# Two gated MLPs whose down-projection takes 16 of 22 row blocks in seven block products instead of eight

## The chip, the cores and the metric

The kernel runs on one core of one Trainium2 chip. A core has five engines with queues of their own: the matrix engine (PE, with its weight loads PEld), the vector engine VectorE (DVE), the scalar engine ScalarE (ACT), GpSimd (POOL), and SyncE (SP), which here only issues DMAs. Operands lie in the on-chip memory SBUF, matmul results in the eight banks of PSUM. The metric is the device time of one execution, in microseconds (us); lower is better.

## The reference

The reference is a trunk of two layers on one sequence of 512 tokens with 1024 features, in float32. Each layer has a mixer, a cross-attention into 256 memory rows, and a gated MLP; each is followed by x <- LayerNorm(alpha * x + f(x)). The change touches the MLP, whose hidden width D_FF is 2816, or 22 blocks of 128:

```python
def conv_ffn(x, w_up, conv_w, conv_b, w_down):
    up = x @ w_up
    a, g = up[..., :D_FF], up[..., D_FF:]
    g = causal_dwconv(g, conv_w) + conv_b
    return (jax.nn.gelu(g) * a) @ w_down
```

Layer 0 mixes with a spatial gate and trailing pooling (`mixer_ab`), layer 1 with a short gated convolution (`mixer_c`).

## The kernel before

**Numbers as pairs.** Every matmul operand is held as a high and a low part in a shorter format (float32r). `split` (L68) makes them: ScalarE copies the value into the high part (L70), VectorE subtracts it from the value for the low part (L71). `mm3` (L132) multiplies two such operands with three matmuls: high x high, high x low, low x high (L133 to L135).

**Weights.** They pass through in chunks of 128 x 1024, 512 KB, in the order of a list written out beforehand, `plan` (L81 to L96). `Weights.load` (L104) takes a raw buffer (4 of them), lets SyncE load the chunk (L117) and splits it into one of 6 ring places (`RING`). `take` hands out the next chunk; `done` (L126), called when the matmuls of a chunk have been written out, loads one more into the oldest place.

**Matmul forms.** In `proj_feat` (L163) weights stand still and activations move, and the result has features on the partitions. In `proj_tok` (L182) the activations stand still, 128 x 128 at a time, and 512 columns of the weights move; the result has tokens on the partitions. The MLP's up-projection uses the first form, its down-projection the second.

**MLP.** The 22 hidden blocks are worked in three groups, `FFN_GROUPS` = 6, 8 and 8 blocks. For a group, `ffn_up` (L500) takes two chunks for each hidden block m (gate and value), runs 24 matmuls for each, and then convolves (ScalarE L371, VectorE L373 twice), applies gelu (ScalarE L509), multiplies (VectorE L510) and splits into the pair of tiles of `Act`. Then `residual_norm` (L229) multiplies the group with its rows of `ffn_w_down`: for each of two column halves n, four PSUM banks, one for each block of 128 tokens, collect the group's blocks, and four additions on VectorE (L246) add them into x, with alpha in the first group. A chunk of `ffn_w_down` covers two row blocks and one column half.

**The last part of a product.** In the last group (`final`) the second column half goes token block by token block: all chunks of that half are held, each token block's products run, are added to x, and the row is normalised (`normalise`, L192: statistics on VectorE, a power on GpSimd in L198, two passes on VectorE in L199 and L201) while the next token block multiplies. Transposes back to feature form (`to_feat`, L218) of the first two token blocks stand inside the products of the third and fourth; those of the last two are emitted by `late` in the next stage. In the last layer the fourth token block is cut into halves of 256 columns, and the rows go out by DMA (L203).

**Order.** Nothing is synchronised by hand. A tile library assigns buffers, places semaphores, and orders each engine's queue; the code's order is its guide. Pools: 11 pairs of activation tiles, 6 ring places, 4 raw buffers, 9 temporaries of 512 columns, 8 PSUM banks.

Of the kernel before, what the change touches and what calls it, by code (L numbers as in the profile page):

```python
# [8 lines left out]
F32 = mybir.dt.float32  # L9
# [5 lines left out]
P = 128  # L15
# [14 lines left out]
RING = 6  # L30
FFN_GROUPS = ((0, 6), (6, 14), (14, 22))
# [4 lines left out]
def kernel(ctx: ExitStack, tc: tile.TileContext, a: dict, out: bass.AP):  # L36
# [24 lines left out]

    def duo(tag="act"):
        pool = apool if tag == "act" else wpool
        h = pool.tile([P, CH], F32R, tag=tag + "h", name=nm(tag + "h"))
        l = pool.tile([P, CH], F32R, tag=tag + "l", name=nm(tag + "l"))
        return h, l

    def split(h, l, src):  # L68
        """h + l == src exactly, each with 12 significant bits."""
        nc.scalar.copy(h, src)  # L70
        nc.vector.tensor_sub(l, src, h.bitcast(F32))  # L71

    def load_split(src, tag):
        raw = rpool.tile([P, CH], F32, tag="raw", name=nm("raw"))
        nc.sync.dma_start(raw, src)
        h, l = duo(tag)
        split(h, l, raw)
        return h, l

    # ---- the weights' chunks, in the order in which the tensor engine meets them  # L80
    plan = []  # L81
    for layer in range(2):
# [11 lines left out]
        for m0, m1 in FFN_GROUPS:  # L94
            plan += [("ffn_w_up", layer, i) for i in range(2 * m0, 2 * m1)]
            plan += [("ffn_w_down", layer, n, i) for n in range(2) for i in range(m0 // 2, m1 // 2)]  # L96

    class Weights:
        """A ring of chunks: take() gives the next one, and done() loads one more in place of the oldest."""

        def __init__(self):
            self.ready, self.loaded, self.taken = [], 0, 0

        def load(self, parts=1, other=None):  # L104
            """Loads a chunk; in parts that alternate with those of other = (source, duo), if it is given."""
# [6 lines left out]
            raws = [rpool.tile([P, CH], F32, tag="raw", name=nm("raw")) for _ in both]  # L112
# [19 lines left out]
    def mm3(ps, lh, ll, rh, rl, start, stop):  # L132
        nc.tensor.matmul(ps, lh, rh, start=start, stop=False)  # L133
        nc.tensor.matmul(ps, lh, rl, start=False, stop=False)  # L134
        nc.tensor.matmul(ps, ll, rh, start=False, stop=stop)  # L135

    # ---- constants
# [11 lines left out]
    wsT = cpool.tile([P, 4, P], F32, tag="wsT", name="wsT")  # L149
    bsb = cpool.tile([P, 4, P], F32, tag="bsb", name="bsb")  # L150

    # ---- activations held as (high, low) pairs, one pair of tiles for two blocks of 128 features
# [9 lines left out]

    def proj_feat(ps, w, xT, cols=slice(0, S)):  # L163
        """ps[features, tokens] = w.T @ xT, w a chunk [P, 8, 128] of the weight's columns."""
# [4 lines left out]
    def proj_batch(keys, xT, late=None):  # L169
        """proj_feat for a few chunks; late() emits the last half of the tokens in xT."""  # L170
# [21 lines left out]
    def normalise(z, stats, g, b, dst=None):  # L192
        """z = (z - mean) * rsqrt(var + eps) * g + b over the free axis."""
# [11 lines left out]
    def load_consts():  # L205
        nc.sync.dma_start(wsT, a["sgu_w"])
# [6 lines left out]
        for t in range(NT):  # L213
            nc.sync.dma_start(xt[t], a["x"][0, t * P : (t + 1) * P, :])

    xt = [xpool.tile([P, D], F32, tag=f"x{t}", name=f"x{t}", bufs=1) for t in range(NT)]

    def to_feat(xT, t):  # L218
        """xT[:, :, block t] = transpose of xt[t]."""
# [8 lines left out]

    def residual_norm(groups, wname, ln, layer, last=False, hooks={}, ahead=None):  # L229
        """x = LayerNorm(alpha * x + sum over groups of act.T @ w), as (transposed x, function that  # L230
        emits the last half of its tokens).
# [381 lines left out]
```

## Time and profile before

| | |
|---|---|
| median of 3 runs | 1361.77 us (1361.37 to 1362.26) |
| span of the profiled execution, first to last instruction | 1359.5 us |
| instructions | 16304 |
| matmuls recorded | 6628 |
| bytes loaded on SyncE's queue | 141.94 MB |

The profile is a record of one execution; the page lists only its span, and the runs' median lies 2.3 us above it. Its views: the page's busy times of each engine and its 40 slices; the chain of work that ended last; the groups of instructions by line, operation and shape, each with count, busy time, mean duration in ns, and the idle time of the engine ahead of it with what ended it; the waits, with total, count and longest; stretches, which give each engine's busy time between two instants; and timelines, which list start, duration, engine, line, tiles and shapes. In a name such as `wl<-raw,wh` the output stands left of the arrow; `wh` and `wl` are the two parts of a ring place, `acth` and `actl` of an activation, `ps` is a PSUM bank, `x` the residual stream. A few per cent of the matmul records may be missing.

### The profile page before, as it was taken

How to read it: one execution, taken by the hardware profiler on the slowest of the kernel's cores; microseconds unless marked ns; L12 is line 12 of the kernel's file. 1: busy time of each engine (PE TensorE's matmuls, PEld its weight loads, DVE VectorE, ACT ScalarE, POOL GpSimd, SP SyncE). 2: the span in 40 equal slices, each digit the busy share in tenths (PEclk: the TensorE clock that was granted, in tenths of full speed). 3: DMA queues.
4: the chain of work that ended last, by engine and by line, in shares of the span. 5: the costliest groups of instructions: out<-in, count | busy, mean ns of one | idle time of the engine just before them, and what ended most of it. 6: DMA issues, size and time to landing. Idle time of an engine off the chain costs nothing.

```text
span 1359.5 us, 16304 instructions
## 1 busy us (share of the span) xinstructions
PE 1347.2 (99%) x6628; PEld 1143.2 (84%) x6628; DVE 736.5 (54%) x998; ACT 465.3 (34%) x663; POOL 48.6 (4%) x68
## 2 busy tenths in 40 slices
PE   8999999999999999999999999999999999999997
PEld 7888888898888888888988888988898888888886
DVE  5768446675444424446744447565674444444436
ACT  5343345234223313332532222354243233313320
POOL 0102000010000000001000001000110000000001
PEclk9999999999999999999999999999999999999999
DMA  8633533133332233332623331442143233332301
GB/s 283 207 124 108 171 120 114 62 104 114 97 105 93 93 97 105 94 93 93 217 93 94 101 101 47 158 152 78 47 153 95 94 98 104 93 93 98 104 32 62
DMA packets 42844, 149.28 MB, mean 110 GB/s; under 512 B 5136, under 2 KB 5264, under 8 KB 42768
## 3 DMA queue, kind: packets, MB, share of 16 engines
q1 hardware_dynamic: 41040, 141.94, 32.7%
q0 software_dynamic: 1728, 6.29, 1.3%
q8 instruction: 52, 0.85, 0.2%
q14 instruction: 24, 0.20, 0.0%
HBM read 146.12 MB, written 2.10 MB: 109 GB/s over the span
## 4 chain that ended last, share of the span: by engine, by line
PE 99%; DMA 0%; DVE 0%; POOLq 0%; DVEq 0%; ACT 0%; issue 0%; SPq 0%
PE ps L133 32%; PE ps L134 32%; PE ps L135 32%; PE ps L223 1%; PE ps L469 1%; PE ps L346 0%; DMA raw<-in_ab_w_v 0%; POOLq L601 0%; DVE x L201 0%; DVEq L601 0%; ACT wh L70 0%; DVE stats L254 0%; DVE x L246 0%; SPq L117 0%; DVE mv L196 0%
## 5 line engine op out<-in xcount | busy, mean ns | idle before, releaser
L71 DVE TENSOR_TENSOR wl<-raw,wh 128x1024 fp32r<-128x1024 f32 (+1 forms) x251 | 304.3, 1212 | 416.7 <-ACT wh L70 406.8
L133 PE MATMUL ps<-acth,wh 128*128 128x512 f32 (+1 forms) x1316 | 478.5, 364 | 0.0
L134 PE MATMUL ps<-actl,wh 128*128 128x512 f32 (+1 forms) x1316 | 478.0, 363 | 0.0
L135 PE MATMUL ps<-acth,wl 128*128 128x512 f32 (+1 forms) x1316 | 478.0, 363 | 0.0
L70 ACT CAST wh<-raw 128x1024 fp32r<-128x1024 f32 (+1 forms) x251 | 262.2, 1045 | 607.6 <-PE ps L134 276.3
L133 PE MATMUL ps<-wh,acth 128*128 128x512 f32 (+1 forms) x712 | 277.3, 390 | 4.6 <-ACT wh L70 4.6
L133 PEld LDWEIGHTS ps<-acth,wh 128*128 128x128 f32 x1316 | 248.4, 189 | 38.9
L135 PEld LDWEIGHTS ps<-acth,wl 128*128 128x128 f32 x1316 | 248.4, 189 | 38.9
L134 PEld LDWEIGHTS ps<-actl,wh 128*128 128x128 f32 x1316 | 248.4, 189 | 38.6
L135 PE MATMUL ps<-wh,actl 128*128 128x512 f32 (+1 forms) x712 | 276.1, 388 | 0.0
L134 PE MATMUL ps<-wl,acth 128*128 128x512 f32 (+1 forms) x712 | 276.0, 388 | 0.0
L133 PEld LDWEIGHTS ps<-wh,acth 128*128 128x128 f32 x712 | 134.1, 188 | 31.5 <-ACT wh L70 4.6
L135 PEld LDWEIGHTS ps<-wh,actl 128*128 128x128 f32 x712 | 134.0, 188 | 27.5
L134 PEld LDWEIGHTS ps<-wl,acth 128*128 128x128 f32 x712 | 134.2, 188 | 27.2 <-DVE wl L71 0.4
L70 ACT CAST acth<-ps 128x256 fp32r<-128x256 f32 (+1 forms) x144 | 63.0, 470 | 121.4 <-PE ps L223 81.9
L198 POOL TENSOR_TENSOR rs<-rs,mhalf 128x1 f32<-128x1 f32 x28 | 40.2, 1437 | 1290.1 <-DVE rs L197 1290.1
L71 DVE TENSOR_TENSOR actl<-ps,acth 128x256 fp32r<-128x256 f32 (+1 forms) x144 | 73.0, 536 | 14.0 <-ACT acth L70 13.6
L510 DVE TENSOR_TENSOR tmp<-tmp,ps 128x512 f32<-128x512 f32 x44 | 30.3, 688 | 80.6 <-PE ps L135 79.2
L246 DVE SCALAR_TENSOR_TENSOR x<-x,ps 128x512 f32<-128x512 f32 (+1 forms) x81 | 54.6, 678 | 31.9 <-PE ps L135 31.6
L373 DVE SCALAR_TENSOR_TENSOR tmp<-ps,convw,tmp 128x511 f32<-128x511 f32 x88 | 65.7, 746 | 1.5
L509 ACT ACTIVATE tmp<-tmp 128x512 f32<-128x512 f32 x44 | 27.8, 632 | 85.9 <-DVE tmp L373 85.9
L70 ACT CAST acth<-tmp 128x512 fp32r<-128x512 f32 x64 | 39.4, 620 | 20.0 <-DVE tmp L330 14.0
(66 smaller groups left out, 549.2 us busy)
## 6 DMA issues: line engine op xcount, KB each, us to landing
raw<-in_ffn_w_up SPq DMA_DIRECT2D x88, 512.0 KB, 3.5
raw<-in_ffn_w_down SPq DMA_DIRECT2D x44, 512.0 KB, 3.5
raw<-in_c_w_in SPq DMA_DIRECT2D x24, 512.0 KB, 3.7
raw<-in_xa_wk SPq DMA_DIRECT2D x16, 512.0 KB, 3.7
raw<-in_xa_wq SPq DMA_DIRECT2D x16, 512.0 KB, 3.9
raw<-in_xa_wv SPq DMA_DIRECT2D x16, 512.0 KB, 3.7
raw<-in_xa_wo SPq DMA_DIRECT2D x16, 512.0 KB, 4.2
raw<-in_ab_w_f SPq DMA_DIRECT2D x8, 512.0 KB, 4.9
```

Of the source, the lines that this page charges most:

```text
L70: nc.scalar.copy(h, src)
L71: nc.vector.tensor_sub(l, src, h.bitcast(F32))
L133: nc.tensor.matmul(ps, lh, rh, start=start, stop=False)
L134: nc.tensor.matmul(ps, lh, rl, start=False, stop=False)
L135: nc.tensor.matmul(ps, ll, rh, start=False, stop=stop)
L198: nc.gpsimd.tensor_tensor(rs, rs, mhalf, op=ALU.pow)
L223: nc.tensor.transpose(ps[:, k * P : (k + 1) * P], xt[t][:, (half * 4 + k) * P : (half * 4 + k + 1) * P], ident)
L246: nc.vector.scalar_tensor_tensor(z, z, ALPHA if gi == 0 else 1.0, ps, op0=ALU.mult, op1=ALU.add)
L373: nc.vector.scalar_tensor_tensor(dst[:, s:], src[:, : S - s], tap(2 - s), dst[:, s:], op0=ALU.mult, op1=ALU.add)
L469: nc.tensor.transpose(ps[:, t * P : (t + 1) * P], es[h][t // 2][:, c0 : c0 + P], ident)
L509: nc.scalar.activation(g, g, AF.Gelu_apprx_tanh)
L510: nc.vector.tensor_mul(g, g, ps[2 * i + 1])
```

## The change

`FFN_GROUPS` becomes 8, 8 and 6 blocks. The groups of 8 are multiplied in another way; the group of 6, as all other products, as before.

**Seven products.** Take two hidden blocks, one even and one odd, and cut everything in two: the tokens into halves of 256, the blocks into the even and the odd one, the columns into halves of 512. The activations are A11 (even, first tokens), A12 (odd, first), A21 (even, last), A22 (odd, last); the weights B11, B12 (even block, first and second column half), B21, B22 (odd block). With

- S1 = A21 + A22, S2 = S1 - A11, S3 = A11 - A21, S4 = A12 - S2
- T1 = B12 - B11, T3 = B22 - B12, T2 = T3 + B11, T4 = B21 - T2

the four results are C11 = A11 B11 + A12 B21; U = A11 B11 + S2 T2; C12 = U + S1 T1 + S4 B22; C21 = U + S3 T3 + A22 T4; C22 = U + S3 T3 + S1 T1. These are seven products where a plain multiplication has eight.

**Activation sums.** `Blocks.new` gives a float32 tile of eight 128 x 256 blocks. The last multiplication of `ffn_up` (L510) writes a block's two token halves straight into it; after the odd block, `finish` makes the four sums on VectorE and splits the seven operands as one of 1792 columns.

**Weight sums.** A group takes 14 chunks in place of 8: for every four hidden blocks two chunks `b11b21` (loaded), one `t1t1` (T1 of both pairs); later two `t2b22` and one `t4t4`; last one `t3t3`. `Weights.fast` loads the halves that it needs (for `b11b21` 768 KB in all, for `t2b22` 1 MB), and makes the T's with `nc.gpsimd` in raw buffers; T1, T4 and T3 stay in raw buffers until their turn in the list. Then `split` puts them into the ring.

**Products.** `fast_product` runs three phases over the pairs of a group, with the PSUM banks X, Y, Z, two each (one for each 128 tokens of a half). First phase: A11 B11 into X, A12 B21 into Z, S1 T1 into Y; then X and Z are added into C11's place of x, Y into C22's. Second phase: S2 T2 on top of X, A22 T4 into new Z banks, S4 B22 on top of Y; then X and Y are added into C12's place, Z into C21's. Third phase: S3 T3 on top of X, which is added into C21's and C22's places.

**Room in SBUF.** The ring has 5 places instead of 6, there are 7 raw buffers instead of 4 and 4 temporaries instead of 9. Activation pairs come from one pool of 12 slots of 8 KB per partition. `mixer_ab` keeps v, u, its padded rows and its constants in such slots (before: temporaries and tiles of their own).

The diff, without the comments that it drops and the moves inside `mixer_ab`:

```diff
-RING = 6
-FFN_GROUPS = ((0, 6), (6, 14), (14, 22))
+RING = 5
+FFN_GROUPS = ((0, 8), (8, 16), (16, 22))
...
-    apool = ctx.enter_context(tc.tile_pool(name="apool", bufs=11))
+    apool = ctx.enter_context(tc.tile_pool(name="apool", bufs=12))
-    rpool = ctx.enter_context(tc.tile_pool(name="rpool", bufs=4))
+    rpool = ctx.enter_context(tc.tile_pool(name="rpool", bufs=7))
-    tpool = ctx.enter_context(tc.tile_pool(name="tpool", bufs=9))
+    tpool = ctx.enter_context(tc.tile_pool(name="tpool", bufs=4))
+    fpool = ctx.enter_context(tc.tile_pool(name="fpool", bufs=1))
...
+    def fast_plan(layer, i0, i1):
+        p = []
+        for i in range(i0, i1, 2):
+            p += [("b11b21", layer, i), ("b11b21", layer, i + 1), ("t1t1", layer, i)]
+        for i in range(i0, i1, 2):
+            p += [("t2b22", layer, i), ("t2b22", layer, i + 1), ("t4t4", layer, i)]
+        return p + [("t3t3", layer, i) for i in range(i0, i1, 2)]
...
+        def fast(self, what, layer, i):
+            w = a["ffn_w_down"][layer]
+            half = [slice(0, 512), slice(512, CH)]
+            def fetch(src):
+                t = raw_tile()
+                nc.sync.dma_start(t[:, : src.shape[-1]], src)
+                return t
+            def both(key):
+                if i % 2 == 0:
+                    self.kept[key] = raw_tile()
+                return self.kept[key][:, half[i % 2]]
+            if what == "b11b21":
+                w0, w1 = fetch(w[0, i]), fetch(w[1, i][:, half[0]])
+                nc.gpsimd.tensor_sub(both("t1"), w1[:, half[0]], w0[:, half[0]])
+                return w0
+            if what == "t2b22":
+                w1, w0, t3 = fetch(w[1, i]), fetch(w[0, i]), both(("t3", i // 2))
+                b12 = t2 = w1[:, half[0]]
+                nc.gpsimd.tensor_sub(t3, w1[:, half[1]], b12)
+                nc.gpsimd.tensor_add(t2, t3, w0[:, half[0]])
+                nc.gpsimd.tensor_sub(both("t4"), w0[:, half[1]], t2)
+                return w1
+            return self.kept.pop({"t1t1": "t1", "t4t4": "t4", "t3t3": ("t3", i // 2)}[what])
...
+            if key[0] not in a:
+                w = duo("w")
+                split(*w, self.fast(*key))
+                self.ready.append(w)
+                return
...
+    class Blocks:
+        A11, A12, A22, S1, S2, S3, S4, A21 = range(8)
...
+        def new(self):
+            f = fpool.tile([P, 8, 256], F32, tag="blocks", name=nm("blocks"))
+            def finish():
+                def sub(to, x, y, op=ALU.subtract):
+                    nc.vector.tensor_tensor(f[:, to, :], f[:, x, :], f[:, y, :], op=op)
+                sub(self.S1, self.A21, self.A22, ALU.add)
+                sub(self.S2, self.S1, self.A11)
+                sub(self.S3, self.A11, self.A21)
+                sub(self.S4, self.A12, self.S2)
+                h, l = (slot()[:, : 7 * 256].rearrange("p (b s) -> p b s", b=7) for _ in range(2))
+                self.pairs.append((h, l))
+                split(h, l, f[:, :7, :])
+            return [f[:, self.A11 :: self.A21, :], f[:, self.A12 : self.A22 + 1, :]], finish
...
+    def fast_product(act, layer, i0, first):
...
+        X, Y, Z = ([ps_tile() for _ in halves] for _ in range(3))
+        for i in range(0, n, 2):
+            b = [weights.take("b11b21", layer, i0 + i + j) for j in range(2)]
+            t1 = weights.take("t1t1", layer, i0 + i)
+            for j in range(2):
+                s, e = i + j == 0, i + j == n - 1
+                for p in halves:
+                    mul(X[p], Blocks.A11, i + j, p, part(b[j], 0), s, e)
+                for p in halves:
+                    mul(Z[p], Blocks.A12, i + j, p, part(b[j], 1), s, e)
+                for p in halves:
+                    mul(Y[p], Blocks.S1, i + j, p, part(t1, j), s, e)
+                weights.done()
+            weights.done()
+        for p in halves:
+            add(p, 0, X[p])
+        for p in halves:
+            add(p, 0, Z[p])
+        for p in halves:
+            add(p + 2, 1, Y[p])
...
+        for i in range(0, n, 2):
+            t3 = weights.take("t3t3", layer, i0 + i)
+            for j in range(2):
+                for p in halves:
+                    mul(X[p], Blocks.S3, i + j, p, part(t3, j), None, i + j == n - 1)
+            weights.done()
+        for m in range(2):
+            for p in halves:
+                add(p + 2, m, X[p])
...
+            if isinstance(act, Blocks):
+                fast_product(act, layer, k0 // 2, gi == 0)
+                continue
```

`mul` runs `mm3` for one of the seven blocks and one 128-token block p; the left-out second phase has the form of the first.

More of the change, by code (lines that the diff above doesn't have):

```diff
@@ L95 @@
             plan += [("ffn_w_up", layer, i) for i in range(2 * m0, 2 * m1)]
-            plan += [("ffn_w_down", layer, n, i) for n in range(2) for i in range(m0 // 2, m1 // 2)]
+            if m1 < NF:
+                plan += fast_plan(layer, m0 // 2, m1 // 2)
+            else:
+                plan += [("ffn_w_down", layer, n, i) for n in range(2) for i in range(m0 // 2, m1 // 2)]
     class Weights:
@@ L130, with mm3 @@
     weights = Weights()
[L132 to L135, printed above, removed]
+    def mm3(ps, lh, ll, rh, rl, start, stop, more=False):
+        nc.tensor.matmul(ps, lh, rh, start=start, stop=False, skip_group_check=more)
+        nc.tensor.matmul(ps, lh, rl, start=False, stop=False, skip_group_check=more)
+        nc.tensor.matmul(ps, ll, rh, start=False, stop=stop, skip_group_check=more)
     ident = cpool.tile([P, P], F32, tag="ident", name="ident")
@@ L205, in load_consts @@
     def load_consts():
+        wsb = slot(F32)
+        wsT, bsb = (wsb[:, j * 512 : (j + 1) * 512].rearrange("p (g i) -> p g i", g=4) for j in range(2))
         nc.sync.dma_start(wsT, a["sgu_w"])
@@ L227, in to_feat, with add, mul, part @@
                 split(h, l, src)
+    def fast_product(act, layer, i0, first):
+        halves = (0, 1)
+        seen = set()
+        def add(t, n, ps):
+            z = xt[t][:, n * 512 : (n + 1) * 512]
+            scale = ALPHA if first and (t, n) not in seen else 1.0
+            seen.add((t, n))
+            nc.vector.scalar_tensor_tensor(z, z, scale, ps, op0=ALU.mult, op1=ALU.add)
+        def mul(ps, block, i, p, w, start, stop):
+            h, l = (v[:, block, p * P : (p + 1) * P] for v in act.pairs[i])
+            mm3(ps, h, l, *w, start is True, stop, start is None)
+        def part(w, j):
+            return [v[:, j * 512 : (j + 1) * 512] for v in w]
+        n = len(act.pairs)
+        X, Y, Z = ([ps_tile() for _ in halves] for _ in range(3))
[18 more added lines that the diff above has]
+            add(p + 2, 1, Y[p])
+        Z = [ps_tile() for _ in halves]
+        for i in range(0, n, 2):
+            b = [weights.take("t2b22", layer, i0 + i + j) for j in range(2)]
+            t4 = weights.take("t4t4", layer, i0 + i)
+            for j in range(2):
+                s, e = i + j == 0, i + j == n - 1
+                for p in halves:
+                    mul(X[p], Blocks.S2, i + j, p, part(b[j], 0), None, e)
+                for p in halves:
+                    mul(Z[p], Blocks.A22, i + j, p, part(t4, j), s, e)
+                for p in halves:
+                    mul(Y[p], Blocks.S4, i + j, p, part(b[j], 1), None, e)
+                weights.done()
+            weights.done()
+        for p in halves:
+            add(p, 1, X[p])
+        for p in halves:
+            add(p + 2, 0, Z[p])
+        for p in halves:
+            add(p, 1, Y[p])
+        for i in range(0, n, 2):
+            t3 = weights.take("t3t3", layer, i0 + i)
+            for j in range(2):
+                for p in halves:
+                    mul(X[p], Blocks.S3, i + j, p, part(t3, j), None, i + j == n - 1)
+            weights.done()
+        for m in range(2):
+            for p in halves:
+                add(p + 2, m, X[p])
@@ L296, in mixer_ab @@
     def mixer_ab(xT):
-        v = [tmp() for _ in range(NT)]
+        vs, us, pads = slot(F32), slot(F32), slot(F32)
+        v = [vs[:, t * 512 : (t + 1) * 512] for t in range(NT)]
         ps = [ps_tile() for _ in range(NT)]
@@ L315, in mixer_ab @@
             (ps,) = proj_batch([("ab_w_f", gi)], xT)
-            cur = tpool.tile([P, PAD + S], F32, tag="pad", name=nm("pad"), bufs=3)
+            cur, *free = [pads[:, j * (PAD + S) : (j + 1) * (PAD + S)] for j in range(3)]
             xb = cur
@@ L321, in mixer_ab @@
             while sh < win:
-                nxt = tpool.tile([P, PAD + S], F32, tag="pad", name=nm("pad"), bufs=3)
+                nxt = free[0]
                 lo += sh
                 nc.vector.tensor_add(nxt[:, lo:], cur[:, lo:], cur[:, lo - sh : PAD + S - sh])
+                free = [cur if cur is not xb else free[1]]
                 cur, sh = nxt, sh * 2
@@ L500, in ffn_up @@
     def ffn_up(layer, xT, late, m0, m1):
-        hid = Act(m1 - m0)
+        fast = m1 < NF
+        hid = Blocks() if fast else Act(m1 - m0)
         m = m0
```

38 lines of the change are left out of this document (27 added, 11 removed).

## The prediction

> **What bounds the kernel now.** I read the page's busy times and chain first, then who waited for whom, then stretches and timelines around the MLP.
>
> ```profile
> span 1359.5 us, 16304 instructions
> PE 1347.2 (99%) x6628; PEld 1143.2 (84%) x6628; DVE 736.5 (54%) x998; ACT 465.3 (34%) x663; POOL 48.6 (4%) x68
> PEclk9999999999999999999999999999999999999999
> PE 99%; DMA 0%; DVE 0%; POOLq 0%; DVEq 0%; ACT 0%; issue 0%; SPq 0%
> ```
>
> The matrix engine (PE) carries the chain that ended last, at full granted clock in every slice. A pipelined PE can look busy while it is not dense, so the waits and the distance between matmuls have to confirm it.
>
> ```profile
> ACT wh L70 <- PE ps L134: 276.3, 111, 4.2
> DVE x L246 <- PE ps L135: 31.6, 26, 6.5
> PE ps L133 <- ACT wh L70: 4.6, 1, 4.6
> 353.30:386.00 32.70, 32.70 (x146) 27.09 (x145) 13.26 (x15) 6.89 (x7) 0.00 (x0) 1.00 0.31 97
> 391.00:478.00 87.00, 87.00 (x386) 72.06 (x385) 41.19 (x48) 32.04 (x40) 0.00 (x0) 1.00 0.31 98
> ```
>
> The one recorded wait of PE above half a microsecond is the 4.6 us at the start. Everybody else waits for PE. The two stretches (columns: stretch, its length, then PE, PEld, DVE, ACT, POOL busy with counts) are the first group's down-projection and the second group's up-projection in layer 0: PE is full, VectorE (DVE) works 41% and 47% of the time, GpSimd not at all. So a removed matmul is worth its distance to the next one, as long as nobody makes PE wait. That distance is not the 0.39 us that a matmul lasts, because matmuls overlap:
>
> ```profile
> 365.47 1.23 DVE L71 TENSOR_TENSOR wl<-raw,wh 128x1024 fp32r<-128x1024 f32 x1 [4.21 <-ACT wh L70]
> 367.78 2.73 DVE L246 SCALAR_TENSOR_TENSOR x<-x,ps 128x512 f32<-128x512 f32 x4 [1.09 <-PE ps L135]
> 370.91 1.22 DVE L71 TENSOR_TENSOR wl<-raw,wh 128x1024 fp32r<-128x1024 f32 x1 [0.40 <-ACT wh L70]
> 376.35 1.23 DVE L71 TENSOR_TENSOR wl<-raw,wh 128x1024 fp32r<-128x1024 f32 x1 [4.22 <-ACT wh L70]
> 381.79 1.22 DVE L71 TENSOR_TENSOR wl<-raw,wh 128x1024 fp32r<-128x1024 f32 x1 [4.21 <-ACT wh L70]
> ```
>
> In the down-projection one weight chunk is freed, and the next split, every 381.79 - 376.35 = 5.44 us, and a chunk feeds 2 row blocks x 4 token blocks x 3 = 24 matmuls: 0.2267 us each. These rows show one more thing. In the code the four additions into x stand behind the last weights.done(), whose split is the row at 370.91; on VectorE they ran before it. The queue is ordered by when work is expected to be ready, not by the code.
>
> **The matmuls removed.** Two row blocks of weights cost 2 x 4 x 2 x 3 = 48 matmuls; as seven products 7 x 2 token blocks x 3 = 42. Sixteen row blocks are 8 pairs, in 2 layers: 8 x 2 x 6 = 96 matmuls, all with 512 moving columns. 96 x 0.2267 = **21.8 us** off the path. Regrouping to 8, 8 and 6 blocks changes no other count.
>
> **What is added on VectorE and ScalarE.** Prices:
>
> ```profile
> L71 DVE TENSOR_TENSOR wl<-raw,wh 128x1024 fp32r<-128x1024 f32 x246 | 300.8, 1223 | 415.5 <-ACT wh L70 405.6 <-PE ps L346 4.2
> L70 ACT CAST wh<-raw 128x1024 fp32r<-128x1024 f32 x246 | 259.1, 1053 | 606.2 <-PE ps L134 276.3 <-PE ps L135 196.6 <-issue 104.2
> L246 DVE SCALAR_TENSOR_TENSOR x<-x,ps 128x512 f32<-128x512 f32 x79 | 53.8, 684 | 31.4 <-PE ps L135 31.1
> L71 DVE TENSOR_TENSOR actl<-tmp,acth 128x512 fp32r<-128x512 f32 x64 | 43.6, 685 | 3.0 <-ACT acth L70 3.0
> L71 DVE TENSOR_TENSOR actl<-ps,acth 128x256 fp32r<-128x256 f32 x80 | 30.6, 417 | 6.4 <-ACT acth L70 6.0
> L510 DVE TENSOR_TENSOR tmp<-tmp,ps 128x512 f32<-128x512 f32 x44 | 30.3, 688 | 80.6 <-PE ps L135 79.2 <-ACT tmp L509 1.4
> ```
>
> A group of 8 blocks now takes 168 matmuls (38.1 us) in three phases: 72 matmuls with 6 chunks (16.3 us), again 72 with 6, and 24 with 2 (5.4 us). Before, it took 8 chunks; now 14. Splits: 14 x 1.223 = 17.1 us. Additions into x: 16 instead of 8, 16 x 0.684 = 10.9. For the last pair of blocks, whose up-projection has just ended: product 0.69, four sums at 0.42 = 1.68, and a split of 1792 columns, from the rows for 512 and 1024 (0.538 per 512 more) 1.223 + 1.5 x 0.538 = 2.03. Together 17.1 + 10.9 + 4.4 = 32.4 of 38.1 us. VectorE goes from 41% to 85% busy in this stretch; ScalarE (14 x 1.05 = 14.7) stays far below. In an up-projection of 87 us VectorE adds 4 x (4 x 0.42 + 2.03 - 2 x 0.685) = 9.4 us to some 41: covered.
>
> The tightest place is the first phase. Before the second phase may add its fourth product into the bank of the third (Y), VectorE must have done 6 splits (7.3), X and Z additions (4 x 0.684 = 2.7), the last pair (4.4) and the Y additions (1.4): 15.9 us. The Y matmuls of the second phase come 12 matmuls in, at 16.3 + 2.7 = 19.0 us. Margin 3.1 us. In the second phase, 6 splits and 6 additions make 11.4 us of 16.3.
>
> **New waits at the phase borders.** The second phase goes on accumulating in X, whose bank VectorE must first have added into x (so again before the third). Within the last 18 matmuls of a phase, X is finished 12 matmuls = 2.7 us before the end, and one addition takes 0.68. If VectorE takes it when it is ready, as at 367.78 above, PE does not wait. Behind it in VectorE's queue stand the weight splits; they have the ring as cover. After the third phase X is busy with four more additions, but six banks of eight are idle, so the next up-projection can start. I take 0.9 us per product for these borders and the first-phase jam together: bounds 0, if all hides, and 4.1, worked out below; it is nearer to 0, as the ledger has a margin. Four products: **+3.6 us**.
>
> **The sums on GpSimd.** Sixteen 128x512 sums per product: 4 for T1, 12 for T2, T3, T4. The trace has no such operation. Nearest rows:
>
> ```profile
> L198 POOL TENSOR_TENSOR rs<-rs,mhalf 128x1 f32<-128x1 f32 x28 | 40.2, 1437 | 1290.1 <-DVE rs L197 1290.1
> masks.py:199 POOL TENSOR_SCALAR_AFFINE_SELECT ident<-ident 128x128 f32<-128x128 f32 x1 | 0.3, 291 | 0.0
> L318 POOL MEMSET pad<- 128x16 f32 x4 | 0.4, 112 | 8.5 <-DVE pad L324 8.5
> ```
>
> The select reads one input of 128 columns: (291 - 112) / 112 columns = 1.6 ns a column, so 512 columns take at least 0.9 us. The power row has two inputs and 1.44 us for one column; all of it as a fixed cost plus 512 x 1.6 ns gives 2.3 us. I take 1.2, close to the select, since an addition is no power. The sums of the second phase's second half are the latest. Their raw buffers come free with the splits of the chunks that the first phase frees from 4.1 us on (18 matmuls), so at about 8 us into the product; six sums follow. T4 must be there at about 23.4 us, as its split has to end by 16.3 + 8.2 + 1.4 = 25.8, when its first matmul is due. That leaves 15 us, 2.5 us a sum. At 1.2 nobody waits for GpSimd: 0 us. [...]
>
> **Loads.**
>
> ```profile
> GB/s 283 207 124 108 171 120 114 62 104 114 97 105 93 93 97 105 94 93 93 217 93 94 101 101 47 158 152 78 47 153 95 94 98 104 93 93 98 104 32 62
> raw<-in_ffn_w_down SPq DMA_DIRECT2D x44, 512.0 KB, 3.5
> ```
>
> Half-matrices are read again for the sums: 4 chunks of 768 KB and 4 of 1 MB, 7.3 MB per product instead of 4.2, so 193 GB/s over 38.1 us. Slices of 207 to 283 GB/s are there already. Seven raw buffers instead of four let loads run ahead. 0 us; without that cover one load costs 3.5.
>
> **Ring of 5 instead of 6.** After a last part with four chunks held, one chunk is ready instead of two.
>
> ```profile
> 284.99 0.28 PE L133 MATMUL ps<-acth,wh 128*128 128x256 f32 x1
> 288.46 0.28 PE L135 MATMUL ps<-acth,wl 128*128 128x256 f32 x1
> 280.22 1.05 ACT L70 CAST wh<-raw 128x1024 fp32r<-128x1024 f32 x1 [1.87 <-PE ps L135]
> 284.20 1.21 DVE L71 TENSOR_TENSOR wl<-raw,wh 128x1024 fp32r<-128x1024 f32 x1
> ```
>
> The MLP starts at 284.99; 29 steps to 288.46 are 0.12 us each, so a chunk's first half lasts 24 x 0.12 = 2.9 us, to 287.9. The first chunk reloaded was split by 284.20 + 1.21 = 285.4. It would now be needed second, at 287.9: still 2.5 us early. 0 us.
>
> **The last end.** Six blocks instead of eight make a token block of the last part 18 x 0.2267 = 4.08 us instead of 5.44.
>
> ```profile
> 1340.69 0.69 DVE L246 SCALAR_TENSOR_TENSOR x<-x,ps 128x512 f32<-128x512 f32 x1 [0.53 <-PE ps L135]
> 1346.13 0.69 DVE L246 SCALAR_TENSOR_TENSOR x<-x,ps 128x512 f32<-128x512 f32 x1 [0.55 <-PE ps L135]
> 1354.90 1.41 DVE L201 SCALAR_TENSOR_TENSOR x<-x,rs,row 128x512 f32<-128x512 f32 x2 [0.46 <-POOL rs L198]
> ```
>
> VectorE idled 0.55 of each 5.44 us there: the normalisation takes 4.9 us, now more than a token block of PE. It falls behind by 0.8 us at each of two blocks, less what it fills into its 0.46 us waits for GpSimd, and this stands behind PE's end: **+1.2 us** (0 to 2.5).
>
> **Sum.** -21.8 + 3.6 + 1.2 = -17.0 us. The profiled execution's span of 1359.5 becomes 1342.5. The median of the runs shown, 1361.77, lies 2.3 above that span, for what is around it, which stays: **1344.8 us**. Own range 1340 (nothing waits) to 1349. Chance 0.60.
>
> **Rival 1: VectorE and GpSimd get in each other's way (0.24).** If a GpSimd sum and a VectorE operation with both inputs in SBUF exclude each other, the six sums that I place in the first phase add 6 x 1.2 = 7.2 us to the 15.9: 23.1 against 19.0, so PE waits 4.1 us per product, 16.4 in all: -21.8 + 16.4 + 1.2 = -4.2, **1357.6 us**. It decides from 3.1 us on, less than half of the 7.2. For it: splits and sums (11 of the 15.9 us) have two SBUF inputs. Against it:
>
> ```profile
> 654.52 1.46 POOL L198 TENSOR_TENSOR rs<-rs,mhalf 128x1 f32<-128x1 f32 x1 [8.32 <-DVE rs L197]
> 655.49 1.22 DVE L71 TENSOR_TENSOR wl<-raw,wh 128x1024 fp32r<-128x1024 f32 x1
> ```
>
> This split began inside the power operation and took its usual 1.22 us. But that operation reads a single column, so it hardly tests a long read. [...]
>
> **Rival 2: the X additions come behind the splits (0.08), slower than before.** At 8 borders PE would wait for the cast (1.05), two splits (2.4) and one addition (0.7), 4.2 us: 8 x 4.2 = 34, -21.8 + 34 + 1.2 = +13, **1375 us**. It decides from 20.6 / 8 = 2.6 us a border. Against it: the rows at 367.78 and 370.91. For it: X's addition then kept nobody waiting, and the jam in the first phase can push it.
>
> **Rival 3: GpSimd is too slow (0.05).** Above 2.5 us a sum each product waits six times the excess; at 3.0 us 4 x 6 x 0.5 = 12, -21.8 + 12 + 4.8 = -5, **1357 us**. My upper bound of 2.3 speaks against it; mutual waiting with VectorE would add to it.
>
> **Rival 4: the gain cancels (0.03).** Rival 1 with 19 to 22 us of waits ends within 1359 to 1364.
>
> **How the numbers follow.** About 0.2%, 2.7 us, is what a measurement of this kernel can tell from no change. Forecast, rival 1 and rival 3 are faster: 0.60 + 0.24 + 0.05, less 0.03 for their worst ends: 0.86. Same: 0.03 + 0.01 of those ends = 0.04. Slower: 0.08 + 0.02 = 0.10. The range from 1339.5 (nothing waits, and measuring) to 1358 (rivals 1 and 3 at their prices) leaves out the slow cases and the ends: about 0.18.
>
> **What would show it.** 96 matmuls fewer. PE rows in the products still 0.2267 us apart; idle time of PE, if any, at the first X or Y matmul of phase two, released by an addition into x: below 1.5 us a product by the forecast, some 4 by rivals 1 and 2. For rival 1, splits in the products longer than 1.22 us, or sums longer when they meet them; for rival 2, the X additions after the splits of the freed chunks; for rival 3, casts of T chunks waiting for GpSimd. Between PE's end and the last output about 1.2 us more than now. I am wrong if PE waits elsewhere: at an up-projection's start, or for a raw buffer.

## The result and the profile after

The changed kernel takes **1373.05 us** (median of 4 runs, 1372.33 to 1373.76), beside 1361.78 for the kernel before (4 runs, 1361.37 to 1362.26): ratio 1.0082, 95% interval 1.0067 to 1.0096. It is slower by 11 us, where 17 less were forecast. From here line numbers are those of the changed kernel: `split` is now L80 and L81, `mm3` L194 to L196, the sums on GpSimd L148 (T1), L153 (T3), L154 (T2) and L155 (T4), an addition of `fast_product` L328.

The head of the page, with the share of each engine in the chain that ended last:

```profile
span 1370.7 us, 16418 instructions
PE 1336.2 (97%) x6526; PEld 1131.4 (83%) x6526; DVE 841.9 (61%) x1102; ACT 498.1 (36%) x671; POOL 152.6 (11%) x132
PE 90%; POOL 4%; DMA 3%; DVE 2%; issue 1%; ACT 1%; POOLq 0%; DVEq 0%; SPq 0%
```

PE's busy time fell by 11 us while the span grew by 11, and 4% of the chain now lies on GpSimd, 3% on DMA. So PE waits. Who waited for whom:

```profile
ACT wh L80 <- POOL raw L154: 21.1, 4, 5.6
PEld ps L194 <- DVE x L328: 20.6, 4, 5.3
PE ps L194 <- DVE x L328: 18.9, 4, 4.9
```

PE waits four times, once in each product, for an addition into x, and a cast of ScalarE waits four times for the sum T2. The first of these waits, in PE's timeline (start, length, instruction, the idle time before it):

```profile
395.53 0.39 PE L196 MATMUL ps<-wh,act 128*128 128x512 f32 x1
400.50 0.80 PE L194 MATMUL ps<-wh,act 128*128 128x512 f32 x1 [4.58 <-DVE x L328]
401.09 0.63 PE L195 MATMUL ps<-wl,act 128*128 128x512 f32 x1
401.52 0.63 PE L196 MATMUL ps<-wh,act 128*128 128x512 f32 x1
```

Two things are lost here: the idle time, and what follows it. From 401.09 on one matmul starts 0.43 us after the other instead of 0.2267. The stretches say why (PEclk, the granted clock, is the third number from the right):

```profile
376.04:421.57 45.53, 40.95 (x169) 33.34 (x168) 33.41 (x32) 16.41 (x15) 14.62 (x8) 0.93 0.48 156
395.00:399.17 4.17, 0.92 (x5) 0.42 (x3) 1.94 (x2) 1.04 (x1) 3.61 (x3) 1.00 0.21 84
399.17:406.00 6.83, 5.50 (x13) 4.34 (x14) 2.50 (x3) 1.04 (x1) 0.00 (x0) 0.50 0.73 240
406.00:421.57 15.57, 15.57 (x69) 12.85 (x69) 10.98 (x13) 6.33 (x6) 0.00 (x0) 1.00 0.57 183
```

The product lasts 45.53 us; its 168 matmuls at 0.2267 would last 38.08. Of the 7.45 us lost, the wait is 400.50 - 395.53 less one step, 4.7, and the half clock behind it 2.7. All four products together: 45.53 + 46.03 + 44.45 + 45.40 against 4 x 38.08, so 29.1 us lost, 19.6 in waits and 9.5 at half clock. Now the cause, in VectorE's timeline:

```profile
384.61 6.78 DVE L81 TENSOR_TENSOR wl<-raw,wh 128x1024 fp32r<-128x1024 f32 x3
391.32 3.06 DVE L328 SCALAR_TENSOR_TENSOR x<-x,ps 128x512 f32<-128x512 f32 x5
394.31 2.00 DVE L81 TENSOR_TENSOR wl<-raw,wh 128x1024 fp32r<-128x1024 f32 x1
398.53 1.31 DVE L81 TENSOR_TENSOR wl<-raw,wh 128x1024 fp32r<-128x1024 f32 x1 [2.23 <-ACT wh L80]
399.77 0.67 DVE L328 SCALAR_TENSOR_TENSOR x<-x,ps 128x512 f32<-128x512 f32 x1
```

Five of the six additions of the first border are done by 394.4. The sixth, that of Y's second token block, stands in the queue behind two splits. Its bank was ready: the 72nd matmul, the last of the first phase, started at 392.1, and yet VectorE sat idle for 2.23 us ahead of the second split. That split belongs to the last T2 chunk, and its cast came late: in ScalarE's and GpSimd's timelines

```profile
397.45 1.04 ACT L80 CAST wh<-raw 128x1024 fp32r<-128x1024 f32 x1 [5.07 <-POOL raw L154]
```

```profile
382.85 2.99 POOL L153 TENSOR_TENSOR raw<-raw 128x512 f32<-128x512 f32 x1 [3.83 <-DMA raw<-in_ffn_w_down]
385.92 2.15 POOL L154 TENSOR_TENSOR raw<-raw,raw 128x512 f32<-128x512 f32 x1
388.15 2.16 POOL L155 TENSOR_TENSOR raw<-raw,raw 128x512 f32<-128x512 f32 x1
393.93 1.29 POOL L153 TENSOR_TENSOR raw<-raw 128x512 f32<-128x512 f32 x1 [3.62 <-DMA raw<-in_ffn_w_down]
395.30 2.12 POOL L154 TENSOR_TENSOR raw<-raw,raw 128x512 f32<-128x512 f32 x1
```

The last T2 sum ended at 397.42. It had waited for its load, the load for a raw buffer that the three sums before it held until 390.3, and those took 7.3 us together. The sum at 393.93, which starts beside additions with one SBUF input, takes 1.29; beside splits and block sums, which have two, a sum takes up to 3.1. Both sides pay, as the groups show (busy, mean ns of one):

```profile
L81 DVE TENSOR_TENSOR wl<-raw,wh 128x1024 fp32r<-128x1024 f32 x270 | 353.5, 1312 | 315.3 <-ACT wh L80 307.1 <-PE ps L510 4.2
L148 POOL TENSOR_TENSOR raw<-raw,raw 128x512 f32<-128x512 f32 x16 | 27.1, 1691 | 269.7 <-DVE wl L81 216.6 <-DMA raw<-in_ffn_w_down 53.0
L154 POOL TENSOR_TENSOR raw<-raw,raw 128x512 f32<-128x512 f32 x16 | 26.9, 1681 | 11.5 <-DMA raw<-in_ffn_w_down 10.6
```

270 splits at 1312 instead of 1223 ns are 24 us more on VectorE; the four sums of each block pair and the activations' splits, against a kernel without weight sums (below), make it 27, nearly 7 per product. GpSimd's 64 sums take 104.1 us, where 64 at 1.29 would take 82.6. Last, the end, in VectorE's timeline (the additions that open a token block, and the last step):

```profile
1347.64 0.69 DVE L408 SCALAR_TENSOR_TENSOR x<-x,ps 128x512 f32<-128x512 f32 x1 [1.12 <-PE ps L196]
1352.47 0.68 DVE L408 SCALAR_TENSOR_TENSOR x<-x,ps 128x512 f32<-128x512 f32 x1
1357.28 0.68 DVE L408 SCALAR_TENSOR_TENSOR x<-x,ps 128x512 f32<-128x512 f32 x1
1365.40 1.41 DVE L288 SCALAR_TENSOR_TENSOR x<-x,rs,row 128x512 f32<-128x512 f32 x2 [0.44 <-POOL rs L285]
```

A token block takes VectorE 4.82 us, and the matmuls of one only 4.08. So VectorE falls behind by 0.7 to 0.8 at each of the last three blocks (the very last, cut into halves, takes PE 4.3 us and VectorE 5.1), 2.3 in all. From PE's last matmul to the end of the span it is now 10.67 us, before 7.64: +3.0. Of these, 2.3 come before VectorE's last row ends, and 0.7 after it. The ledger of the spans: -21.8 + 29.1 + 3.0 is 10.3 of the 11.2 us; the other 0.9 lie in the kernel's first 30 us (below).

### The profile page after: what moved, and what is told of

It reads as the page before. It is cut to its first block, busy times and chain, and to the rows that moved or that the text cites. A ratio compares the mean times of both kernels' runs of the same rounds, so it can differ in the third digit from the quotient of the medians.

```text
span 1370.7 us, 16418 instructions
## 1 busy us (share of the span) xinstructions
PE 1336.2 (97%) x6526; PEld 1131.4 (83%) x6526; DVE 841.9 (61%) x1102; ACT 498.1 (36%) x671; POOL 152.6 (11%) x132
## 4 chain that ended last, share of the span: by engine, by line
PE 90%; POOL 4%; DMA 3%; DVE 2%; issue 1%; ACT 1%; POOLq 0%; DVEq 0%; SPq 0%
PE ps L194 29%; PE ps L195 29%; PE ps L196 29%; DMA raw<-in_ffn_w_down 3%; POOL raw L154 1%; PE ps L313 1%; POOL raw L153 1%; DVE wl L81 1%; POOL raw L155 1%; ACT wh L80 1%; PE ps L633 1%; POOL rs L285 0%; DVE x L288 0%; PE ps L510 0%; DMA raw<-in_ab_w_v 0%
## 5 line engine op out<-in xcount | busy, mean ns | idle before, releaser
L81 DVE TENSOR_TENSOR wl<-raw,wh 128x1024 fp32r<-128x1024 f32 (+1 forms) x275 | 356.9, 1300 | 315.9 <-ACT wh L80 307.6
L80 ACT CAST wh<-raw 128x1024 fp32r<-128x1024 f32 (+1 forms) x275 | 287.4, 1045 | 562.8 <-PE ps L195 263.4
L194 PE MATMUL ps<-act,wh 128*128 128x512 f32 (+1 forms) x1316 | 478.5, 364 | 0.0
L195 PE MATMUL ps<-act,wh 128*128 128x512 f32 (+1 forms) x1316 | 478.0, 363 | 0.0
L196 PE MATMUL ps<-act,wl 128*128 128x512 f32 (+1 forms) x1316 | 478.0, 363 | 0.0
L194 PE MATMUL ps<-wh,act 128*128 128x512 f32 (+1 forms) x678 | 269.4, 397 | 23.9 <-DVE x L328 18.9
L195 PEld LDWEIGHTS ps<-act,wh 128*128 128x128 f32 x1316 | 248.4, 189 | 38.9
L196 PEld LDWEIGHTS ps<-act,wl 128*128 128x128 f32 x1316 | 248.3, 189 | 38.9
L194 PEld LDWEIGHTS ps<-act,wh 128*128 128x128 f32 x1316 | 248.4, 189 | 38.7
L195 PE MATMUL ps<-wl,act 128*128 128x512 f32 (+1 forms) x678 | 266.8, 394 | 0.0
L196 PE MATMUL ps<-wh,act 128*128 128x512 f32 (+1 forms) x678 | 266.6, 393 | 0.0
L194 PEld LDWEIGHTS ps<-wh,act 128*128 128x128 f32 x678 | 130.1, 192 | 52.3 <-DVE x L328 20.6
L195 PEld LDWEIGHTS ps<-wl,act 128*128 128x128 f32 x678 | 130.3, 192 | 26.8 <-DVE wl L81 0.4
L196 PEld LDWEIGHTS ps<-wh,act 128*128 128x128 f32 x678 | 129.8, 191 | 27.2
L80 ACT CAST act<-ps 128x256 fp32r<-128x256 f32 (+1 forms) x144 | 62.9, 470 | 120.3 <-PE ps L313 79.2
L81 DVE TENSOR_TENSOR act<-ps,act 128x256 fp32r<-128x256 f32 (+1 forms) x144 | 73.0, 535 | 13.4 <-ACT act L80 13.0
L148 POOL TENSOR_TENSOR raw<-raw,raw 128x512 f32<-128x512 f32 x16 | 27.1, 1691 | 269.7 <-DVE wl L81 216.6
L81 DVE TENSOR_TENSOR act<-blocks,act 128x1792 fp32r<-128x1792 f32 x16 | 33.5, 2092 | 23.7 <-ACT act L80 23.7
```

Source lines behind the costliest of these rows:

```text
L148: nc.gpsimd.tensor_sub(both("t1"), w1[:, half[0]], w0[:, half[0]])
L194: nc.tensor.matmul(ps, lh, rh, start=start, stop=False, skip_group_check=more)
L195: nc.tensor.matmul(ps, lh, rl, start=False, stop=False, skip_group_check=more)
L196: nc.tensor.matmul(ps, ll, rh, start=False, stop=stop, skip_group_check=more)
```

## The experiments

**Theory.** The sixth addition is stuck in VectorE's order behind a split that waits, through a cast, for GpSimd. GpSimd's and VectorE's mutual blocking makes that split late. **Rival A:** the blocking makes VectorE itself too slow (rival 1 of the prediction); the order does not matter. **Rival B:** the loads, the ring of five or the four temporaries slow the rest as well.

**Additions first.** In the code the six additions move ahead of the last two `weights.done()`. On VectorE one instruction per product changes its place: the sixth addition stands two places earlier.

```diff
                     mul(Y[p], Blocks.S1, i + j, p, part(t1, j), s, e)
+                if e:
+                    ... (the six additions)
                 weights.done()
             weights.done()
-        ... (the six additions)
...
```

> One edit: the first phase's six additions stand in the code ahead of the last two weight loads. On VectorE this moves one instruction in each of the four products: the last addition of Y stands before two splits instead of behind them. Theory (queue place): the four waits of 4.7 to 5.1 us vanish and with them the half-speed matmuls behind them, 29.1 us in all, so 1373.05 - 29.1 = 1344 us, with no wait of the matrix engine over 0.5 us in a product. Rival (too much work on VectorE): the wait moves to a later split or addition, over 1365 us. Rival (sums too slow): the matrix engine waits for the T2 chunk itself some 4 us later, over 1360 us.

**1344.11 us** (4 runs, 1342.72 to 1344.46) against 1361.73: ratio 0.9867 (0.9851 to 0.9884). The products last 38.10 to 38.27 us, PE has no wait in them. VectorE's timeline, then a row of the waits:

```profile
392.17 3.66 DVE L328 SCALAR_TENSOR_TENSOR x<-x,ps 128x512 f32<-128x512 f32 x6
395.76 1.52 DVE L81 TENSOR_TENSOR wl<-raw,wh 128x1024 fp32r<-128x1024 f32 x1
399.54 4.87 DVE L81 TENSOR_TENSOR wl<-raw,wh 128x1024 fp32r<-128x1024 f32 x4 [2.27 <-ACT wh L80]
```

```profile
ACT wh L80 <- POOL raw L154: 21.4, 4, 5.5
```

The T2 cast waits as long as before (21.4 us in all, 21.1 in the changed kernel) and VectorE idles as long in front of it. Only nobody that PE waits for is queued behind it. Rival A falls: with nearly the same blocking (splits 1299 ns) the products lose 0.5 us in all instead of 29.1. This version beats both kernels.

**Y ahead of Z.** Another way to the same end: in the first phase Y's matmuls and additions come before Z's.

```diff
-                for p in halves: mul(Z[p], ...)
                 for p in halves: mul(Y[p], ...)
+                for p in halves: mul(Z[p], ...)
...
```

> The changed kernel with Y's matmuls ahead of Z's in the first phase, and its additions likewise. Y is then complete 6 matmuls earlier, and its last addition stands on VectorE ahead of the split of the last T2 chunk; behind that split stand only the additions of Z, whose banks nobody takes up again in this product. Theory (queue place): no waits over 0.5 us in the products, about 1344 us. Rival (VectorE's load): waits remain, over 1360 us.

1351.13 us (one run), between the two expectations. No matmul waits for an addition any more, but now some wait for splits:

```profile
PE ps L195 <- DVE wl L81: 5.6, 7, 1.3
```

In the first product these are 0.5 and 1.3 us, for T1 chunks, which the new order needs 6 matmuls earlier, and for a T4 chunk, whose sums now come later (the last T2 sum starts at 397.76 instead of 395.30). The other products are much alike: they last 39.89 to 40.26 us, 8.0 us in all over four times 38.08. So the order was the cause of the 5 us waits, but this order spends GpSimd's margin.

**No sums.** T1, T3 and T4 are loaded from `ffn_w_down` as they are, T2's place keeps B12: the same bytes and splits, and no sum. The halves that only the sums read have no raw buffer here, so there is also more room for loads.

```diff
+            def direct(key, s):
+                nc.sync.dma_start(both(key), s)
...
-                nc.gpsimd.tensor_sub(both("t1"), w1[:, half[0]], w0[:, half[0]])
+                direct("t1", w[1, i][:, half[0]])
...
```

> The weight sums on GpSimd are left out: the same bytes are loaded straight into the places of T1, T3 and T4, and T2 stays B12, so the output is not the reference's. VectorE's order is that of the changed kernel, with the last Y addition behind two splits. Theory (a queue place that hurts only because the T2 chunk is late): the splits ahead of that addition are done about 2.5 us after the phase's end, the addition 0.7 later, and its matmuls come 3.4 us after the phase's end, so waits below 0.5 us and about 1344 us. Splits in the products back at 1.22 us. Rival (the place alone, two splits and two casts, is enough): waits of 2 us or more remain in each product, over 1355 us. Rival (too much work on VectorE without GpSimd's part): likewise over 1355.

1342.54 us (1341.75 to 1342.83), ratio 0.9858 (0.9844 to 0.9873); products 38.08, and the splits are back at their time of before:

```profile
L81 DVE TENSOR_TENSOR wl<-raw,wh 128x1024 fp32r<-128x1024 f32 x270 | 329.5, 1222 | 310.1 <-ACT wh L80 297.1 <-DMA raw<-in_xa_wk 4.2 <-PE ps L511 4.2
```

VectorE's order is that of the changed kernel here. So its order alone costs nothing; it needs a T2 chunk that is late. Whether it is the sums or the raw buffers that make it late, this version cannot tell; the next one keeps the buffers.

**Small sums.** 16 of the 512 columns are summed and the rest of T1, T3 and T4 is set to zero: GpSimd stays in the chain of loads and buffers.

```diff
-                nc.gpsimd.tensor_sub(t3, w1[:, half[1]], b12)
...
+                nc.gpsimd.memset(t3, 0.0)
...
+                nc.gpsimd.tensor_sub(t3[:, c], w1[:, 512:528], b12[:, c])
...
```

> The changed kernel with all its loads and buffers and its order on VectorE, but each weight sum makes only 16 of its 512 columns (the rest of T1, T3 and T4 is set to zero, of T2 left as B12, so the output is not the reference's). A chain of load and small sums then takes some 3.6 + 1.2 us a chunk. Theory (the last T2 chunk is late by the sums' length, not by the raw buffers alone): that chunk's sum is done some 6 us before the phase ends, no waits of the matrix engine over 0.5 us in the products, about 1343.5 us. Rival (buffers and loads alone make it late): waits of 2 us or more stay, over 1355 us. Splits of weight chunks back near 1.22 us, as zeroing reads nothing.

1342.68 us (one run); products 38.08 to 38.11; splits 1222 ns. The sixth addition (L333 is its line here) is still behind its two splits, in 2.44 us:

```profile
391.64 2.44 DVE L81 TENSOR_TENSOR wl<-raw,wh 128x1024 fp32r<-128x1024 f32 x2
394.00 0.68 DVE L333 SCALAR_TENSOR_TENSOR x<-x,ps 128x512 f32<-128x512 f32 x1
```

It is the duration of the sums that makes the split late, not that GpSimd has a part in the chain.

**Eight raw buffers** instead of seven (two temporaries instead of four), all else as in the changed kernel.

```diff
-    rpool = ctx.enter_context(tc.tile_pool(name="rpool", bufs=7))
+    rpool = ctx.enter_context(tc.tile_pool(name="rpool", bufs=8))
...
-    tpool = ctx.enter_context(tc.tile_pool(name="tpool", bufs=4))
+    tpool = ctx.enter_context(tc.tile_pool(name="tpool", bufs=2))
```

> The changed kernel with eight raw buffers instead of seven (and two temporaries instead of four, for the room; what that costs is outside the MLP products). Theory (the loads of a T2 chunk wait for a raw buffer that the sums before it hold, so that load and sums alternate): with one more buffer a load runs beside the sums before it, the last T2 is ready some 3.5 us earlier, the waits in the products shrink from 4.7 to 5.1 us to below 1.5 and half-speed matmuls go: products of 38 to 40 us. Rival (the sums' own length decides): the products stay within 1 us of 44.5 to 46.0 us.

1348.76 us (one run); products 39.32 to 39.70.

```profile
392.71 3.73 DVE L81 TENSOR_TENSOR wl<-raw,wh 128x1024 fp32r<-128x1024 f32 x2
396.36 0.67 DVE L328 SCALAR_TENSOR_TENSOR x<-x,ps 128x512 f32<-128x512 f32 x1
```

The last T2 sum now ends at 393.13, 16.9 us into the product and 4.5 earlier than in the changed kernel, and no split waits for it. What is left, 1.1 to 1.5 us of wait a product, is the blocking on VectorE: the two splits ahead of the sixth addition take 3.73 us here and 2.44 with small sums. So of the 4.7 to 5.1 us of the changed kernel some 3.6 came by way of the raw buffer and its load, and some 1.3 from VectorE's own slowing. These short waits also left the clock alone: its mean over the run is 0.998, as without sums, where the changed kernel has 0.989.

**Sums twice.** The version with the additions first, each sum made twice in a row.

```diff
-                nc.gpsimd.tensor_sub(t3, w1[:, half[1]], b12)
...
+                for _ in range(2):
+                    nc.gpsimd.tensor_sub(t3, w1[:, half[1]], b12)
...
```

> The first experiment's kernel with every sum on GpSimd made twice (the second time to the same value). If sums and VectorE's operations with two SBUF inputs hold each other up, the mean split of a weight chunk rises by about as much again as sums raised it (1.223 to 1.312 us), to 1.40; if not, it stays at 1.31. By the theory that the sums' chain (load, sums, load, sums) is late by itself, the T2 chunks now come late for their own matmuls: at some 13 us for each of four, against 4.1 us of matmuls each, 10 to 20 us of waits per product, 1385 to 1425 us. If sums have much room, less than 5 us per product, below 1365.

1417.47 us (one run); products 56.15 to 57.13. PE waits 11.7 to 13.5 us at one place of each product, now for a cast (L200 is a matmul here, L334 an addition):

```profile
PE ps L200 <- ACT wh L80: 56.2, 5, 13.3
PE ps L200 <- DVE x L334: 5.0, 4, 1.8
```

This is GpSimd as the bound: rival 3 of the prediction. The weight splits alone, 1332 ns in the mean instead of 1299, grew less than the expected 1.40, but they are not all that has two SBUF inputs on VectorE. The four activation sums grew more (additions first, then sums twice):

```profile
L238 DVE TENSOR_TENSOR blocks<-blocks 128x256 f32<-128x256 f32 x64 | 29.8, 465 | 1.7
L244 DVE TENSOR_TENSOR blocks<-blocks 128x256 f32<-128x256 f32 x64 | 40.4, 631 | 1.7
```

Without weight sums they take 424 ns. With these and the activations' splits (2154 and 2298 ns, without weight sums 2027), VectorE's lengthening is 25.6 us with the additions first and 47.5 here, for 103.4 and 202.3 us of sums on GpSimd: nearly in proportion. It is not fixed by the sums' time alone: with Y ahead of Z, 101 us of sums lengthen VectorE by only 16.7.

**All but the products.** Layout, ring of five, temporaries and groups of the change, but the plain product for all groups.

```diff
-            if m1 < NF:
+            if False:
...
-        fast = m1 < NF
+        fast = False
```

> Everything of the change but the seven products: groups of 8, 8 and 6 blocks, ring of 5, seven raw buffers, four temporaries, the new places of activations; eight products as before. Theory: only the start (1.0 us later) and the end (2.9 us longer after the last matmul) remain, so 1361.8 + 3.9 = 1365.7 us. Rival (the smaller ring or the fewer temporaries cost in the stages between): over 1368 us, with waits of the matrix engine there.

1364.42 us (10 runs), ratio 1.0018 (1.0009 to 1.0027). PE has no wait between start and end; rival B falls, for all stages but the products themselves. What is left is the end.

**Groups only.** The kernel before with groups of 8, 8 and 6 blocks.

```diff
-FFN_GROUPS = ((0, 6), (6, 14), (14, 22))
+FFN_GROUPS = ((0, 8), (8, 16), (16, 22))
```

> The kernel before with the groups of hidden blocks as 8, 8 and 6 instead of 6, 8 and 8, and nothing else. Theory (the longer end is VectorE's normalisations, 4.82 us per token block against 18 matmuls of 4.08): 10 to 10.8 us from the last matmul to the end instead of 7.6, so 1361.8 + 2.7 = 1364.5 us. Rival (the longer end comes from the new buffers, or from the seven products before it): end of 7.6 us, 1361.8 us.

1364.56 us (11 runs) against 1361.70 (15): ratio 1.0019 (1.0010 to 1.0028), +2.9 us. From PE's last matmul to the end it is 9.89 us, 2.25 more than the 7.64 of before, and the last VectorE rows are those of the changed kernel, 4.8 us a token block. So the regrouping alone accounts for 2.25 of the 3.0 us at the changed kernel's end. The other 0.7 shows in some kernels with the products (additions first, small sums) and not in others (no sums and eight raw buffers: 9.9 to 10.0). VectorE has no part in it: in all of these its last row ends 6.7 us after PE's last matmul. Where the 0.7 shows, the last output DMA lands 2.6 to 2.7 us after its issue, elsewhere 2.0 to 2.1; why it is longer there, no run explains.

**A lighter end.** The version with the additions first; in the last layer the second pass of the normalisation of three token blocks goes to ScalarE (scale) and GpSimd (add).

```diff
...
+            if light:
+                nc.scalar.activation(z[:, c], z[:, c], AF.Copy, scale=rs[:, 0:1])
+                nc.gpsimd.tensor_add(z[:, c], z[:, c], b[:, c])
...
```

> The first experiment's kernel, and in the last layer's last normalisation, for the first three token blocks, the second pass (times the row factor, plus b) on ScalarE and GpSimd instead of VectorE. Theory (after the last matmul VectorE still has the normalisations to catch up, 4.82 us per token block against 4.08 of matmuls): VectorE now has some 3.0 us per block and keeps up; the 10.6 us from the last matmul to the end become 7.8 as in the kernel before, so 1344.1 - 2.8 = 1341.3 us. Rival (GpSimd is late with its addition or its power operation): no gain, 1344 us or more.

1344.07 us (1343.39 to 1344.32), ratio 0.9867 (0.9851 to 0.9884), the same as without it; the end stays at 10.75 us. The rival held, again by order in a queue: the last power operation, on which the output depends, stands behind GpSimd's additions.

```profile
1333.02 3.33 POOL L290 TENSOR_TENSOR x<-x,row 128x512 f32<-128x512 f32 x2 [0.83 <-ACT x L289]
1336.31 0.54 POOL L285 TENSOR_TENSOR rs<-rs,mhalf 128x1 f32<-128x1 f32 x1
```

**The kernel before once more**, unchanged, for the kernel's start.

> The kernel before once more, for its start. In its first profile the clock rose to full at 8.1 us; in the five later ones of changed kernels at 10.1 to 11.3. If the change delays the start, it rises near 8.1 again and the first product takes 23.7 us; if it is chance, it may rise anywhere from 8.1 to 11.5 and that product takes 23.7 to 25.0 us.

1361.99 us (one run). Its first 96 matmuls take 24.24 us; in the first profile of the kernel before they took 23.70, in the changed kernel 24.43, in the other runs 23.68 (small sums) to 25.02 (additions first). So the 0.9 us of the ledger lie within what the start varies from profile to profile; they are not shown to belong to the change. These durations go with the moment at which the granted clock first rises to full: 8.10 us in the first profile of the kernel before, 9.46 in this one, 10.05 in the changed kernel, 11.27 with the additions first.

## Why the prediction was wrong, step by step

**Right: the matmuls.** -21.8 us. With the additions first the products last 38.10 to 38.27 us where 38.1 was worked out, and the whole kernel gains 17.6 us: -21.8, +0.5 in the products, +3.0 at the end, and 0.7 within what the start varies. That this version's 1344.11 us lies so near the forecast of 1344.8 is luck: the borders were put at 3.6 and cost 0.5, the end at 1.2 and cost 3.0.

**Wrong: "At 1.2 nobody waits for GpSimd: 0 us."** This is the step that failed, and not by the size of a sum alone. It asked when PE needs T4, and set a deadline of 23.4 us into the product. GpSimd met it: the last T4 sum ended at 398.77, 22.7 us after the product's start at 376.04 (23.2 at most in the others). But PE isn't the only one that waits for a sum. The split of a T chunk stands in VectorE's queue, and VectorE took it in order: in the rows from 394.31 to 399.77 it sat idle for 2.23 us ahead of the split, with an addition behind it whose bank was ready. So behind the split of the last T2 chunk stood the addition that PE needed 19.7 us into the product (its 88th matmul). The deadline that counted was that of the next instruction behind the split; the T2 sum ended 21.4 us into the product. The price was low too: a sum took 1.29 us beside operations with one SBUF input, but 1.63 in the mean of 64 and up to 3.1, not 1.2.

**Wrong with it: "If VectorE takes it when it is ready … PE does not wait."** The rows that supported this, at 367.78 of the kernel before, showed an addition ahead of a split that stands earlier in the code. In the changed kernel five of six additions are placed so, and the sixth isn't. The ledger of 15.9 us counted the work of VectorE ahead of Y's additions; it held no split of the second phase and no time in which VectorE waits. The border term of 0.9 us a product measured 7.3.

**Sized too small: the price of a wait.** The rivals priced PE's waits alone. Behind waits of 4.7 us and more came a stretch at half clock that cost 1.6 to 3.0 us again, 9.5 of the 29.1 us.

**Rival 1 was half right.** Sums do lengthen splits: no sums, small sums and full ones give splits of 1222, 1222 and 1312 ns. On VectorE this costs nearly 7 us a product, of which 4.8 to 5.1 lie in the first phase, where rival 1 put 7.2. The 3.1 us of margin and the 4.1 us of wait worked out from it don't describe what happened, as nearly the same blocking (4.8 to 5.1 us with the additions first, too) costs almost nothing when the order is right. The price, 1357.6, missed too. Rival 2 came nearest in time (1375) and in place: an addition behind splits. But it named X's additions and eight borders of 4.2 us; it was one of Y's, at four. That its time lies so near is luck. Rival 3's sign, casts that wait for GpSimd, showed as well (21.1 us), but PE never waited for a T chunk itself.

**Wrong: loads at nothing.** "Seven raw buffers … let loads run ahead": they did not where it counted. A raw buffer held by a sum made the next load wait, and an eighth buffer (with two temporaries fewer) takes 24 of the changed kernel's 1373 us away.

**Sized too small: the end.** +1.2 (0 to 2.5); the regrouping measured 2.25, and the changed kernel 3.0, with 0.7 in its last output DMA. The step let VectorE fall behind at two token blocks and fill its waits for GpSimd; the trace shows it behind by 0.7 to 0.8 at three.

**Right at zero:** the ring of five and the temporaries (all but the products, less the regrouping: 1364.42 against 1364.56).

What stays open: how much of the 3.6 us by way of the raw buffer is the lengthening of the sums by VectorE, and how much their 1.29 us each. Small sums remove both. The rows of the first product give an estimate for it alone: three sums of 7.3 us together, where three at 1.29 are 3.9, so 3.4 us of lengthening ahead of the late load.

## What to carry to other kernels

Whoever moves work to a slower engine sets the deadline not by the final consumer but by the first instruction that stands behind a waiting one in any queue between; list that queue in its real order, and put the instruction on which the bounding engine waits ahead of those that wait for the slow one. Work on VectorE and GpSimd with two SBUF inputs was longer on both when it met: splits of 1.22 us took up to 2.3, sums of 1.29 up to 3.1. It has to be priced so. A wait of the matrix engine of 4.7 us and more cost a stretch at half clock on top; waits of up to 1.5 us did not.

## What the runs showed of the hardware

**Half clock behind a wait.** In the changed kernel the granted clock fell to 0.50 for 3.41 or 6.83 us (multiples of the same 3.41) behind each wait of 4.7 us and more, and not behind the 1.1 to 1.5 us of the kernel with eight raw buffers (mean clock 0.998). In the kernel with sums twice a wait of 1.81 us brought it once. As a stretch:

```profile
538.70:542.20 3.50, 3.45 (x10) 2.83 (x11) 2.89 (x5) 0.00 (x0) 2.62 (x3) 0.65 0.33 136
```

The wait ended at 538.75; the clock was full until 539.74 and half for 3.41 us. In the changed kernel's profile the ten changes of the clock lie whole multiples of 3.413 us apart: 114 of them from the rise at 10.05 to the first fall at 399.17, 37 from the rise at 406.00 to the next fall at 532.29. In the 3.41 us ahead of the four falls in its products PE was idle for 76 to 100%; in the 3.41 us behind them it was idle for 38 to 68% where the half clock lasted 6.83 us, and for 6% where it lasted 3.41. By what rule the clock falls was not shown: no run shifts a wait on purpose.

**GpSimd and VectorE take turns.** In the changed kernel a 128x512 sum took GpSimd 1.28 to 1.30 us where it met no VectorE operation with two SBUF inputs (26 of the 64), up to 3.1 where it met one, and the splits that met a sum took up to 2.3 us instead of 1.22. In the rows of the first product, the split that began at 394.31, inside the sum of 393.93 to 395.22, ended at 396.31, 1.09 us after it; the T2 sum that began inside that split, at 395.30, ended at 397.42, 1.11 us after it. Over the changed kernel, 104.1 us of sums lengthened VectorE's work by 27 us, and were themselves lengthened by 21.5. One row of the kernel before stands against it: the power operation at 654.52, on a single column, beside which a split took its usual 1.22 us. That row was a poor test, as the prediction said; small sums of 16 columns left the splits at 1222 ns too.
